# Two SwiGLU phases with five Strassen-Winograd pairs instead of four, the first pair's weight sums made earlier and kept in device memory

## The chip, the cores and the metric

One core of one Trainium2 chip. The metric is device time in microseconds (us) of one execution of the whole program. The engines named are those of the profile: PE (TensorE, matrix products), ACT (ScalarE), DVE (VectorE), POOL (GpSimd), and SP, which here only issues transfers.

## The reference

A decoder of two layers, 256 tokens of width 1024 in float32. Each layer is a half-step SwiGLU, an attention and another half-step SwiGLU: stick-breaking attention in the first layer, native sparse attention (NSA) in the second, whose keys and values are made between the layers. Cut to what the change touches:

```python
D_FF = -(-8 * D_MODEL // (3 * 256)) * 256      # 2816

def _swiglu(x, w_in, w_out):
    a, b = jnp.split(x @ w_in, 2, axis=-1)
    return (jax.nn.silu(a) * b) @ w_out

    for layer in range(DEPTH):
        h = h + 0.5 * _swiglu(_rmsnorm(h, ffn1_norm[layer]), ffn1_w_in[layer], ffn1_w_out[layer])
        hn = _rmsnorm(h, mix_norm[layer])
        ...
        h = h + 0.5 * _swiglu(_rmsnorm(h, ffn2_norm[layer]), ffn2_w_in[layer], ffn2_w_out[layer])
        if layer == N_A_LAYERS - 1:
            kvs = _nsa_shared_kv(h, kv_norm, nsa_w_kv, nsa_k_norm, ...)
    return h
```

## The kernel before

The program runs through phases in this order: f10 (first SwiGLU), stick (attention), f20 (second SwiGLU), kv (shared keys and values), f11 (third SwiGLU, with the compression of keys and values as side work), nsa (attention), f21 (fourth SwiGLU).

**Products.** A float32 product is made of three matmuls (`mm3`, L283 to L285): high part by high part, high by low, low by high. So each weight is split in two. A weight unit of 128x1024 (512 KB) is loaded by SP's queue into a ring of raw buffers (`ring`; five wraw, and three more in f10, f20 and f21), ScalarE copies its high part wh (L219), VectorE subtracts for the low part wl (L221), and the pair stands in a ring of six, two more in the phases named, until TensorE has read it. `pump` makes the next unit's split, `take` hands it out, `done` frees it, and `room` says how far ahead `pump` may go. The units are worked through in one list, `units`, written at build time in the order in which TensorE takes them.

**SwiGLU.** The 2816 columns are 11 blocks of 256, each with its gate columns beside it. A block made directly is 48 matmuls of 128x512 on 4 units. Its two gate products g (one per 128 tokens, L588 or L590) are then transposed (gTp, L598) and split into gTh and gTl (L604). The output product takes 22 chunks of 12 matmuls on one unit each, for which the transposed g must be there; its accumulators take four of the eight PSUM banks.

**Pairs.** Two blocks can be made as a pair, by the Strassen-Winograd scheme: seven products of 12 matmuls instead of eight, on sums of the inputs (`sums_of_h`, four subtractions hg at L646 to L649 and their splits, sums, at L644, once per phase) and on sums of weights. Of a pair's four weight tiles (two units each, b11, b12, b21, b22) products 1, 3 and 2 take b11, b22 and b21 as they are. Product 5 takes b11+b12, product 6 that plus b22, product 4 that plus b21, and product 7 b12+b22. VectorE makes the first three sums in tiles named keep (L229, six adds of 128x1024 per pair); the fourth comes from a plain load of b12 and an accumulating transfer of b22 on GpSimd's queue.

**Order.** Every engine's order is fixed at build time. `FAST` writes out a phase: a number is a direct block, a tuple is a pair with a pattern. In a pattern a digit is one of the seven products, c a chunk of the output product, m the transposes of one finished block, f and g the halves of a direct block inside a pair, s a step of side work, t and x the points where the transfers for product 7 of this pair and the next pair are issued. Blocks before the first tuple run first; chunks that no pattern holds run after the last pair. `chunk_order` gives the order in which blocks enter the output product.

## Time and profile before

| | us |
|---|---|
| median of 3 runs (lowest, highest) | 1001.96 (1001.72, 1002.34) |
| the profiled execution | 1002.48 |
| its span | 1000.7 |
| PE busy in it | 988.1 |
| DVE busy | 867.6 |
| ACT busy | 690.4 |
| POOL busy | 109.1 |

The TensorE clock granted was 1.0 throughout. A span is the time from the first to the last instruction of the profiled execution; what lies around it is 1.8 us. In the rows below, a row of a window gives its bounds and length, then the busy time and count of PE, PEld (weight loads), DVE, ACT and POOL, the granted clock, the share of the transfer engines and GB/s. A row of a timeline gives start and duration, engine, line, operation, output and inputs with their shapes, how many instructions in a row it holds, and in brackets the idle time before it with what ended it. A row of waits gives total, count and longest, in us. By TensorE's instructions f20 begins at 306.6, kv at about 483, f11 at 518, nsa at 714 and f21 at 822.

### The profile page before, as it was taken

The page shows a single profiled execution, that of the slowest core. Times are in us where ns is not written, and L with a number is a line of the kernel's source. Part 1 is how long each engine was busy: PE and PEld are TensorE (multiplying, and loading weights), DVE is VectorE, ACT ScalarE, POOL GpSimd, SP SyncE. Part 2 cuts the span into 40 slices and gives each one's busy share as a digit, 9 for nine tenths or more (in the row PEclk, how much of TensorE's full clock was granted, in tenths as well). Part 3 has the DMA queues.
Part 4 walks back from the last instruction along what each step waited for, and adds up shares of the span by engine and source line. Part 5 has one row for each costly group of instructions (what it writes and reads, how often), then busy time and mean ns, then how long its engine had stood idle before and what let it go on. Part 6 is the DMA issues. An engine that isn't in the chain of part 4 may idle for free.

```text
span 1000.7 us, 14046 instructions
## 1 busy us (share of the span) xinstructions
PE 988.1 (99%) x4985; PEld 822.2 (82%) x4985; DVE 867.6 (87%) x1157; ACT 690.4 (69%) x1083; POOL 109.1 (11%) x164
## 2 busy tenths in 40 slices
PE   9999999999999999999999999999999999999998
PEld 6787887899978888888887887888887888888887
DVE  7899999878869999997777788898799859999993
ACT  6676767577857677676565775666589857767771
POOL 0000000000000000000116400000046501000000
PEclk9999999999999999999999999999999999999999
DMA  9988774554336877665544584766350167687831
GB/s 333 346 245 254 227 219 136 178 171 131 125 124 231 265 238 231 234 190 175 198 156 154 196 301 148 227 211 211 119 187 23 43 224 213 204 248 229 244 110 43
DMA packets 55366, 193.67 MB, mean 194 GB/s; under 512 B 6272, under 2 KB 7296, under 8 KB 55296
## 3 DMA queue, kind: packets, MB, share of 16 engines
q1 hardware_dynamic: 51552, 180.03, 53.3%
q0 software_dynamic: 3456, 12.58, 7.3%
q8 instruction: 39, 0.64, 0.3%
q14 instruction: 31, 0.25, 0.1%
q10 hardware_dynamic: 288, 0.16, 0.1%
HBM read 191.70 MB, written 1.05 MB: 193 GB/s over the span
## 4 chain that ended last, share of the span: by engine, by line
PE 68%; issue 12%; DVE 7%; DMA 5%; ACT 4%; POOL 3%; SPq 0%; ACTq 0%; DVEq 0%; POOLq 0%
PE o L283 7%; PE o L285 6%; PE o L284 6%; PE c L283 5%; PE c L285 5%; PE c L284 5%; DVE wl L221 3%; DMA wraw<-in_f1i 2%; PE a L285 2%; PE a L283 2%; PE a L284 2%; PE cu L283 2%; PE cu L285 2%; PE cu L284 2%; DMA keep<-in_f1i 2%
## 5 line engine op out<-in xcount | busy, mean ns | idle before, releaser
L221 DVE TENSOR_TENSOR wl<-wraw,wh 128x1024 fp32r<-128x1024 f32 (+2 forms) x302 | 364.2, 1220 | 41.7 <-ACT wh L219 39.4
L219 ACT ACTIVATE wh<-wraw 128x1024 fp32r<-128x1024 f32 (+1 forms) x304 | 313.6, 1046 | 89.8 <-PE o L285 39.9
L219 ACT ACTIVATE wh<-keep 128x1024 fp32r<-128x1024 f32 x112 | 118.1, 1059 | 72.9 <-DVE keep L229 25.6
L221 DVE TENSOR_TENSOR wl<-keep,wh 128x1024 fp32r<-128x1024 f32 x112 | 133.9, 1220 | 11.1 <-ACT wh L219 10.4
L229 DVE TENSOR_TENSOR keep<-keep,wraw 128x1024 f32<-128x1024 f32 x80 | 97.5, 1219 | 2.5 <-DMA wraw<-in_f1i 1.9
L283 PE MATMUL o<-wh,gTh0f 128*128 128x512 f32 x192 | 76.4, 398 | 0.0
L284 PE MATMUL o<-wl,gTh0f 128*128 128x512 f32 x192 | 74.8, 390 | 0.0
L285 PE MATMUL o<-wh,gTl0f 128*128 128x512 f32 x192 | 74.7, 391 | 0.0
L283 PE MATMUL a<-wh,hT_f 128*128 128x512 f32 x176 | 69.9, 397 | 0.0
L285 PE MATMUL a<-wh,hT_f 128*128 128x512 f32 x176 | 68.9, 392 | 0.0
L284 PE MATMUL a<-wl,hT_f 128*128 128x512 f32 x176 | 68.6, 390 | 0.0
L283 PE MATMUL o<-wh,gTh1f 128*128 128x512 f32 (+1 forms) x160 | 63.7, 398 | 0.0
L284 PE MATMUL o<-wl,gTh1f 128*128 128x512 f32 (+1 forms) x160 | 62.0, 387 | 0.0
L285 PE MATMUL o<-wh,gTl1f 128*128 128x512 f32 (+1 forms) x160 | 61.3, 388 | 0.0
L441 POOL TENSOR_TENSOR rstd<-rss,mhalf 128x1 f32<-128x1 f32 x12 | 7.7, 642 | 376.2 <-DVE rss L439 376.2
L283 PE MATMUL c<-wh,hT_f 128*128 128x512 f32 x120 | 47.0, 391 | 0.0
L285 PE MATMUL c<-wh,hT_f 128*128 128x512 f32 x120 | 46.7, 389 | 0.0
L284 PE MATMUL c<-wl,hT_f 128*128 128x512 f32 x120 | 46.7, 389 | 0.0
L285 PEld LDWEIGHTS o<-wh,gTl0f 128*128 128x128 f32 x192 | 36.0, 188 | 8.0 <-DVE gTl0f L604 0.2
L283 PEld LDWEIGHTS o<-wh,gTh0f 128*128 128x128 f32 x192 | 36.1, 188 | 7.6 <-ACT vcBh L1233 0.3
L284 PEld LDWEIGHTS o<-wl,gTh0f 128*128 128x128 f32 x192 | 36.1, 188 | 7.1
L285 PEld LDWEIGHTS a<-wh,hT_f 128*128 128x128 f32 x176 | 33.0, 188 | 7.1
(352 smaller groups left out, 2439.3 us busy)
## 6 DMA issues: line engine op xcount, KB each, us to landing
wraw<-in_f1i SPq DMA_DIRECT2D x76, 512.0 KB, 4.5
wraw<-in_f2i SPq DMA_DIRECT2D x72, 512.0 KB, 4.5
wraw<-in_f1o SPq DMA_DIRECT2D x44, 512.0 KB, 4.6
wraw<-in_f2o SPq DMA_DIRECT2D x44, 512.0 KB, 4.8
wraw<-in_sbqk SPq DMA_DIRECT2D x16, 512.0 KB, 3.4
keep<-in_f2i SPq DMA_DIRECT2D x16, 512.0 KB, 4.2
keep<-in_f2i POOLq DMA_DIRECT2D x16, 512.0 KB, 5.5
keep<-in_f1i SPq DMA_DIRECT2D x12, 512.0 KB, 4.5
```

Source lines behind the costliest of these rows:

```text
L219: nc.scalar.activation(hi[:, 0:n], raw[:, 0:n], AF.Copy)
L221: e.tensor_tensor(lo[:, 0:n], raw[:, 0:n], hi[:, 0:n].bitcast(F32), op=OP.subtract)
L229: nc.vector.tensor_tensor(t, y, raw, op=OP.add)
L283: nc.tensor.matmul(o, xh, wh, start=start, stop=False, skip_group_check=True)
L284: nc.tensor.matmul(o, xh, wl, start=False, stop=False, skip_group_check=True)
L285: nc.tensor.matmul(o, xl, wh, start=False, stop=stop, skip_group_check=True)
L441: nc.gpsimd.tensor_tensor(r[:, 0:1], s, mhalf[:, 0:1], op=OP.pow)
```

## The change

f20 and f21 have made blocks 0, 1 and 4 directly (4 inside the first pair) and the pairs (2,3), (5,6), (7,8) and (9,10). They now make block 0 directly and the pairs (1,2), (3,4), (5,6), (7,8) and (9,10). f10 and f11 keep their patterns.

The first pair of f20 and of f21 reads all four weight sums (two units each, eight of 512 KB per phase) from tiles in device memory, as ordinary weight units. Its VectorE adds and its product 7's transfers go. The sums are made earlier:

- for f20 by transfers alone, during the attention (`early_sums`): 4 loads and 8 stores on SP's queue and 8 accumulating transfers on GpSimd's, through four tiles es, one step per `pump` from the twelfth unit of the attention on;
- for f21 by VectorE in kv and f11 (`Early` units, inserted in the unit list from the twelfth unit of kv on): 8 loads, 8 adds of 128x1024 (L191 after) and 8 stores.

Besides this, block 0 of f20 and f21 accumulates in the PSUM banks z, the keep tiles of f11 are opened before kv, and f21's raw ring starts at another place (`turn`). Over the whole program TensorE has 4954 matmuls instead of 4978, VectorE 414 splits instead of 402, 90 adds into keep instead of 84 and 6 into wraw instead of 4, and 32 adds x instead of 28, SP 398 transfers instead of 358 and GpSimd 32 instead of 24.

```diff
@@ -24,10 +24,10 @@
 LOW = 100
 
 
...
-        "f20": (0,1,(2, "1mft5tg36m7xx24", 4), (5,"mc1mccct5ct3cc67xx24"),(7,"mc1mct5ct3cc67xx24"),(9,"mc1mct5t3c6724")),
...
-        "f21": (0,1,(2, "1mft5tg36m7xx24", 4), (5,"mc1mccct5ct3cc67xx24"),(7,"mc1mct5ct3cc67xx24"),(9,"mc1mct5t3c6724"))}
...
+        "f20": (0,(1,"1m25c36m7xxc4"),(3,"m1cmct5t367xxcc24"),(5,"m1mct5t3c67xx24"),(7,"mc1cmt5cct3c67xx24"),(9,"m1mct5t3cc6724")),
...
+        "f21": (0,(1,"1m25c36m7xxc4"),(3,"m1mct5ct3c67xx24"),(5,"mc1mct5ct3c67xx24"),(7,"mc1mct5ct3c67xx24"),(9,"mc1mct5t3c6724"))}
 
 
 def chunk_order(l):
...
@@ -100,12 +107,15 @@
         self.raw, self.hi, self.lo = {}, {}, {}
         self.on_pool = ()
         self.keep, self.kept, self.missed, self.waiting, self.held = None, {}, 0, [], {}
-        self.limit = len(units)
+        self.limit, self.turn, self.owed = len(units), 0, 0
+        self.jobs, self.jobs_from = [], 0
         self.spans, self.extra = [], None
         self.nr = self.nl = self.ns = self.nt = self.nd = 0
 
     def ring(self, u):
-        more = self.extra is not None and self.wide(u) and self.nr % 8 in (1, 4, 7)
+        if self.spans and u == self.spans[-1][0]:
+            self.turn = 6 - self.nr
+        more = self.extra is not None and self.wide(u) and (self.nr + self.turn) % 8 in (1, 4, 7)
         pool, b = (self.extra, 3) if more else (self.pool, self.raws)
         self.nr += 1
         return pool.tile([P, 1024], F32, tag="xraw" if more else "wraw", bufs=b, name=f"wraw{u}")
@@ -127,7 +137,7 @@
         if self.nl >= len(self.units):
             return
         x = self.units[self.nl]
-        if not isinstance(x, Sum):
+        if not isinstance(x, (Sum, Early)):
             self.load_part(0, 1)
             return
         if self.keep is None:
@@ -173,11 +183,35 @@
     def apart(self, u):
         return any(i + 6 <= u < j and (u - i) % 4 == 3 for i, j in self.spans)
 
+    def skip(self, u):
+        return u < len(self.units) and isinstance(self.units[u], Early)
+
+    def early(self, x, u):
+
+        add = lambda t, y: self.nc.vector.tensor_tensor(t, t, y, op=OP.add)
+        k, keep = self.kept[x.key], None
+        y = self.raw.pop(u, None)
+        if x.step == 1:
+            keep, self.held[x.key] = self.held[x.key], y
+            add(keep, y)
+        elif x.step == 2:
+            add(k, self.held.pop(x.key))
+        else:
+            add(k, y)
+            if x.step == 0:
+                self.held[x.key] = y
+            else:
+                del self.kept[x.key]
+        self.nc.sync.dma_start(x.store, k if keep is None else keep)
+
     def room(self, u, slack):
-        if u >= self.nd + self.bufs + 2 * self.wide(u) - slack:
+        if self.skip(u):
+            return True
+        early = sum(self.skip(v) for v in range(self.nd, u))
+        if u >= self.nd + self.bufs + 2 * self.wide(u) - slack + early:
             return False
         n = sum(self.apart(v) for v in range(self.nd, u))
-        return n < 2 if self.apart(u) else u - self.nd - n < self.bufs
+        return n < 2 if self.apart(u) else u - self.nd - n - early < self.bufs
 
     def pair_of(self, u):
         if self.apart(u):
@@ -206,6 +240,18 @@
         while self.nl <= u:
             self.load()
         nc = self.nc
+        if self.skip(u):
+            prio = self.tc.cur_priority
+            self.tc.cur_priority = prio + low
+            self.early(x, u)
+            self.tc.cur_priority = prio
+            self.ns += 1
+            self.owed += 1
+            if x.step > 1:
+                while self.owed:
+                    self.load()
+                    self.owed -= 1
+            return True
         n = x.shape[-1] if isinstance(x, bass.AP) else 1024
         hi, lo = self.hi[u], self.lo[u] = self.pair_of(u)
         if not isinstance(x, Sum):
@@ -235,13 +281,20 @@
         self.tc.cur_priority = prio
         self.ns += 1
         self.load()
+        if self.jobs and u >= self.jobs_from:
+            self.jobs.pop(0)()
         return True
 
     def done(self, n=1):
 
-        self.nd += n
+        for _ in range(n):
+            while self.skip(self.nd):
+                self.nd += 1
+            self.nd += 1
 
     def take(self):
+        while self.skip(self.nt):
+            self.nt += 1
         u = self.nt
         while self.ns < u + 1:
             assert self.pump(0)
@@ -286,6 +339,49 @@
 
 
     units = []
+    dr = ctx.enter_context(tc.tile_pool(name="dr", bufs=1, space=bass.MemoryType.DRAM))
+    stored = {}
+
+    def store(l, n):
+
+        j = [e[0] for e in FAST[l] if isinstance(e, tuple)][n]
+        stored[l, j] = [[dr.tile([P, 1024], F32, name=f"s{l}{j}{y}{i}") for i in range(2)] for y in range(4)]
+
+    def early_units(l):
+
+        j = next(j for x, j in stored if x == l)
+        at = stored[l, j]
+        v = []
+        for i in range(2):
+            b = lambda y, k: a[l[:2] + "i" + l[2]][4 * (j + y) + 2 * k + i]
+            key = ("p", "t", i)
+            v += [Early(key, 0, at[0][i], b(0, 0), b(1, 0)), Early(key, 1, at[1][i], None, b(1, 1)),
+                  Early(key, 2, at[2][i]), Early(key, 3, at[3][i], None, b(0, 1))]
+        return v
+
+    def early_sums(pool, l, j):
+
+        at = stored[l, j]
+        b11, b12, b21, b22 = [[a[l[:2] + "i" + l[2]][4 * (j + y) + 2 * k + i] for i in range(2)]
+                              for k in range(2) for y in range(2)]
+        x, y = [[pool.tile([P, 1024], F32, tag=f"es{z}{i}", bufs=1, name="es") for i in range(2)] for z in range(2)]
+
+        def move(*pairs):
+            for t, src in pairs:
+                for i in range(2):
+                    tc.keep_in_program_order(nc.sync.dma_start(t[i], src[i]))
+
+        def plus(*pairs):
+            for t, src in pairs:
+                for i in range(2):
+                    nc.gpsimd.dma_start(t[i], src[i], accum_op=OP.add)
+
+        jobs = []
+        for gap, f, *y_ in zip((1, 1, 1, 2, 2, 2, 1, 3, 1, 4), (move, move, plus, plus, move, plus, move, move, plus, move),
+                             (((x, b11),), ((y, b12),), ((x, b12),), ((y, b22),), ((at[0], x),), ((x, b22),), ((at[1], y),),
+                              ((at[2], x),), ((x, b21),), ((at[3], x),))):
+            jobs += [lambda: None] * (gap - 1) + [lambda f=f, z=y_[0]: f(*z)]
+        return jobs
 
     def fast(l):
 
@@ -307,18 +403,22 @@
             z = pairs.index(j)
             b11, b21, b12, b22 = b(j, 0), b(j, 1), b(j + 1, 0), b(j + 1, 1)
             key = [(j, "t", i) for i in r]
+            at = stored.get((l, j))
             third = lambda z, i: (pairs[z], 2, i)
             kept = lambda last=False: [Sum(key[i], last=last) for i in r]
-            plus = [(third(z, i), b22[i], True) for i in r]
+            plus = [(third(z, i), b22[i], True) for i in r] if at is None else []
             own = l != "f11"
             ahead = []
-            if own and z == 0:
+            if own and z == 0 and at is None:
                 for i in r:
                     also(i - 2, (third(0, i), b12[i], False))
-            if own and z + 1 < len(pairs):
+            if own and z + 1 < len(pairs) and (l, pairs[z + 1]) not in stored:
                 ahead = [(third(z + 1, i), b(pairs[z + 1] + 1, 0)[i], False) for i in r]
             for ch in pat:
-                if ch == "1":
+                if at is not None and ch in "1536724":
+                    x = {"1": b11, "3": b22, "2": b21, "5": at[0], "7": at[1], "6": at[2], "4": at[3]}[ch]
+                    v += [Unit(x[i]) for i in r]
+                elif ch == "1":
                     v += [Unit(b11[i], key=key[i], of=third(z, i)) if own else Sum(key[i], load=b11[i], join=b12[i])
                           for i in r]
                 elif ch in "56":
@@ -356,13 +456,18 @@
         fast(l)
         spans.append((n, len(units)))
 
+    store("f20", 0)
+    store("f21", 0)
+
     wide("f10")
 
     units[0:8] = [units[4 * (i % 2) + i // 2] for i in range(8)]
+    st0 = len(units)
     for i in range(2):
         units.extend(a["sbv"][j] for j in range(4 * i, 4 * i + 4))
         units.extend(a["sbqk"][j] for j in range(8 * i, 8 * i + 8))
     add("sbo"), wide("f20")
+    kv0 = len(units)
     add("kv")
     f1i1 = fast("f11")
     units.extend(f1i1[:4 * CMP_J])
@@ -372,6 +477,11 @@
         units.extend(f1i1[4 * CMP_J + 2 * i:4 * CMP_J + 2 * i + 2])
     units.extend(f1i1[4 * CMP_J + 8:])
     add("nsi0"), add("nsi1")
+    k = kv0 + 12
+    for i, x in enumerate(early_units("f21")):
+        k += (0, 2, 2, 2)[i % 4]
+        units.insert(k, x)
+        k, cw = k + 1, cw + 1
     nso = len(units)
     add("nso"), wide("f21")
     W = Weights(tc, wp, units, raws=5, bufs=6)
@@ -778,7 +888,7 @@
                 twin()
             else:
                 for j in range(j0):
-                    o = accs("a")
+                    o = accs("a") if j or l == "f11" else [zbank("a") for _ in range(2)]
                     for i, f in enumerate(proj_block(512, hT, j == 0, post, o)):
                         f()
                         if j and i == 1:
@@ -852,6 +962,8 @@
             vp = [sp.tile([P, 2, 8, P], R, name=f"vp{i}") for i in range(2)]
             rB = sp.tile([P, 512], F32, name="rBqk")
             qkT, z, spx, wx = {}, {}, {}, {}
+            W.jobs = [f for l, j in stored if l == "f20" for f in early_sums(sp, l, j)]
+            W.jobs_from = st0 + 12
 
             def v_evac(i, o):
                 for t in range(2):
@@ -1575,6 +1687,7 @@
         fp1 = st["fp"] = fes.enter_context(ffn_pool("f11"))
         qg = st["qg"] = kp.tile([P, DH], F32, name="qg")
         nc.vector.tensor_scalar(qg, vec[:, V_QN:V_QN + DH], 0.125, None, op0=OP.mult)
+        W.open(fp1)
         side = kv_phase(n3, rs, post, st)
         n5 = HT("m1")
         rs, post = ffn("f11", n4, rs, post, [(5, n5)], side, fp1,
```

VectorE at the start of f20's first pair, before. hg and sums are the sums of inputs, wl a unit's low part, keep a weight sum, gTl0f the low part of transposed gates, g a gate product:

```order
L649 SCALAR_TENSOR_TENSOR hg<-hg 128x512
L644 TENSOR_TENSOR sums<-hg,sums 128x512 x3
L221 TENSOR_TENSOR wl_3374<-wraw_3327,wh_3373 128x1024
L221 TENSOR_TENSOR wl_3388<-wraw_3347,wh_3387 128x1024
L229 TENSOR_TENSOR keep<-keep,wraw_3327 128x1024
L604 TENSOR_TENSOR gTl0f_3446<-gTp,gTh0f_3445 128x512
L229 TENSOR_TENSOR keep<-keep,wraw_3347 128x1024
L221 TENSOR_TENSOR wl_3406<-wraw_3361,wh_3405 128x1024
L590 TENSOR_TENSOR g<-a_3397,sil 128x256
L221 TENSOR_TENSOR wl_3422<-wraw_3379,wh_3421 128x1024
L221 TENSOR_TENSOR wl_3435<-keep,wh_3434 128x1024
```

The same place after:

```order
L759 SCALAR_TENSOR_TENSOR hg<-hg 128x512
L754 TENSOR_TENSOR sums<-hg,sums 128x512 x3
L267 TENSOR_TENSOR wl_3412<-wraw_3369,wh_3411 128x1024
L714 TENSOR_TENSOR gTl0f_3483<-gTp,gTh0f_3482 128x512
L267 TENSOR_TENSOR wl_3424<-wraw_3387,wh_3423 128x1024
L267 TENSOR_TENSOR wl_3459<-wraw_3399,wh_3458 128x1024
L700 TENSOR_TENSOR g<-c_3450,sil 128x256
L267 TENSOR_TENSOR wl_3471<-wraw_3415,wh_3470 128x1024
L267 TENSOR_TENSOR wl_3493<-wraw_3427,wh_3492 128x1024
L267 TENSOR_TENSOR wl_3505<-wraw_3462,wh_3504 128x1024
L267 TENSOR_TENSOR wl_3522<-wraw_3474,wh_3521 128x1024
```

The keep adds are gone, and splits stand in their place.

VectorE in kv, around the statistics kss of the keys (kvb is the keys' work tile, Vl a small low part of the values):

```order
L457 TENSOR_TENSOR hT_f_5008<-hg,hT_f_5008 128x4x128
L1071 SCALAR_TENSOR_TENSOR Vl<-kv_5082,rstd,Vh 128x2x64
L646 TENSOR_TENSOR hg<-hg 128x512
L221 TENSOR_TENSOR wl_5179<-wraw_5125,wh_5178 128x1024
L1071 SCALAR_TENSOR_TENSOR Vl<-kv_5083,rstd,Vh 128x2x64
L1092 TENSOR_REDUCE kss<-kvb 128x16
L1071 SCALAR_TENSOR_TENSOR Vl<-kv_5083,rstd,Vh 128x2x64
L1093 TENSOR_SCALAR kss<-kss 128x16
L221 TENSOR_TENSOR wl_5205<-wraw_5137,wh_5204 128x1024
```

After:

```order
L1183 SCALAR_TENSOR_TENSOR Vl<-kv_5156,rstd,Vh 128x2x64
L191 TENSOR_TENSOR keep<-keep,wraw_5280 128x1024
L1183 SCALAR_TENSOR_TENSOR Vl<-kv_5157,rstd,Vh 128x2x64
L267 TENSOR_TENSOR wl_5275<-wraw_5260,wh_5274 128x1024
L1183 SCALAR_TENSOR_TENSOR Vl<-kv_5157,rstd,Vh 128x2x64
L1204 TENSOR_REDUCE kss<-kvb 128x16
L267 TENSOR_TENSOR wl_5295<-wraw_5262,wh_5294 128x1024
L1205 TENSOR_SCALAR kss<-kss 128x16
L191 TENSOR_TENSOR keep<-keep,wraw_5264 128x1024
```

Between the two kss instructions a wl stands now instead of a Vl, and early adds (L191) before and after.

VectorE further on, around hT_xb, which GpSimd's work on kvb and ScalarE release:

```order
L221 TENSOR_TENSOR wl_5321<-wraw_5220,wh_5320 128x1024
L1154 TENSOR_TENSOR hT_xb<-kvb,hT_xb 128x16x64
L221 TENSOR_TENSOR wl_5333<-wraw_5267,wh_5332 128x1024
L221 TENSOR_TENSOR wl_5382<-wraw_5279,wh_5381 128x1024
L604 TENSOR_TENSOR gTl0f_5344<-gTp,gTh0f_5343 128x512
L590 TENSOR_TENSOR g<-a_5300,sil 128x256
L221 TENSOR_TENSOR wl_5394<-wraw_5324,wh_5393 128x1024
L590 TENSOR_TENSOR g<-a_5301,sil 128x256
```

After:

```order
L267 TENSOR_TENSOR wl_5419<-wraw_5404,wh_5418 128x1024
L756 TENSOR_TENSOR hg<-hg 128x512
L757 TENSOR_TENSOR hg<-hg 128x512
L1266 TENSOR_TENSOR hT_xb<-kvb,hT_xb 128x16x64
L758 SCALAR_TENSOR_TENSOR hg<-hg 128x512
L267 TENSOR_TENSOR wl_5464<-wraw_5430,wh_5463 128x1024
L267 TENSOR_TENSOR wl_5486<-wraw_5432,wh_5485 128x1024
L714 TENSOR_TENSOR gTl0f_5442<-gTp,gTh0f_5441 128x512
L759 SCALAR_TENSOR_TENSOR hg<-hg 128x512
L700 TENSOR_TENSOR g<-a_5392,sil 128x256
L267 TENSOR_TENSOR wl_5528<-wraw_5467,wh_5527 128x1024
L700 TENSOR_TENSOR g<-a_5393,sil 128x256
```

Two hg now stand ahead of hT_xb that stood earlier, and two behind it, ahead of the first g.

More of the change, by code (lines that the diff above doesn't have):

```diff
@@ L24 @@
 LOW = 100
-FAST = {"f10": (0, 1, 2, (3, "cccm1ctc5ct367xx24"), (5,"mc1mct5ct3c67xx24"),(7,"mc1mct5ct3c67xx24"),(9,"mc1mct5t36724")),
[3 rows of a table removed]
+FAST = {"f10": (0,1,2,(3,"cccm1ctc5ct367xx24"),(5,"mc1mct5ct3c67xx24"),(7,"mc1mct5ct3c67xx24"),(9,"mc1mct5t36724")),
[3 rows of a table added]
 def chunk_order(l):
@@ L91, in __init__ @@
         self.more = ()
+class Early:
+    def __init__(self, key, step, store, load=None, join=None):
+        self.key, self.step, self.store, self.load, self.join = key, step, store, load, join
 class Weights:
```

2 rows, old and new, of the table FAST are left out of this document.

## The prediction

> **What bounds the kernel now.** First the engines' busy shares, then the chain that ended last, then TensorE's list of waits.
>
> ```profile
> PE 988.1 (99%) x4985; PEld 822.2 (82%) x4985; DVE 867.6 (87%) x1157; ACT 690.4 (69%) x1083; POOL 109.1 (11%) x164
> PE 68%; issue 12%; DVE 7%; DMA 5%; ACT 4%; POOL 3%; SPq 0%; ACTq 0%; DVEq 0%; POOLq 0%
> PE gTp L598 <- DVE g L590: 1.0, 1, 1.0
> PE n L284 <- DVE wl L221: 0.9, 1, 0.9
> PE c L283 <- ACT cp L686: 0.4, 1, 0.4
> ```
>
> TensorE is busy in 988.1 of the span's 1000.7 us, and its waits are single ones of a microsecond or less. It bounds the kernel, so matmuls that go are time that goes, as long as VectorE, second at 87%, keeps the weights split ahead of it. By stretches (columns: length, then busy time of PE, PEld, DVE, ACT and POOL, clock, DMA share, GB/s) the cover is thinner than 87% suggests:
>
> ```profile
> 306.60:466.80 160.20, 160.19 (x728) 131.90 (x727) 156.17 (x171) 116.39 (x145) 7.91 (x9) 1.00 0.75 233
> 822.05:980.50 158.45, 158.44 (x720) 130.49 (x719) 152.79 (x167) 113.74 (x141) 7.99 (x9) 1.00 0.68 203
> 94.18:174.09 79.91, 79.53 (x357) 64.19 (x357) 77.81 (x88) 58.33 (x74) 3.52 (x4) 1.00 0.68 199
> 391.48:425.18 33.70, 33.70 (x154) 27.74 (x153) 32.67 (x34) 24.28 (x29) 1.72 (x2) 1.00 0.77 234
> 383.32:388.76 5.44, 5.44 (x26) 4.50 (x25) 3.93 (x5) 2.13 (x2) 0.00 (x0) 1.00 0.79 270
> ```
>
> The first two are the changed phases f20 and f21: VectorE is busy for 156.17 of 160.20 and 152.79 of 158.45 us, and TensorE still never waits. The third is three pairs of the unchanged f10, the fourth one pair of f20, the fifth two products of it.
>
> **Matmuls.** The last window holds 24 starts of 128x512 matmuls (two more only touch its edges), so 5.44/24 = 0.2267 us each. Two blocks alone are 2 x 48 of them; as a pair they are 7 x 12 = 84. Each phase turns blocks 1 and one other from direct into a pair, so each saves 12 x 0.2267 = 2.72 us: 5.44 us in both. The transposes stay, four per pair. This is all that the change can give.
>
> **VectorE's queue against TensorE's.** The cost is in what VectorE must do per microsecond of TensorE.
>
> ```profile
> 571.24 5.75 DVE L221 TENSOR_TENSOR wl<-wraw,wh 128x1024 fp32r<-128x1024 f32 x5
> 320.70 1.89 DVE L644 TENSOR_TENSOR sums<-hg,sums 128x512 fp32r<-128x512 f32 x3
> 548.19 0.42 DVE L590 TENSOR_TENSOR g<-a,sil 128x256 f32<-128x256 f32 x1
> 322.50 2.35 DVE L221 TENSOR_TENSOR wl<-wraw,wh 128x1024 fp32r<-128x1024 f32 x2
> 329.69 0.39 PE L284 MATMUL c<-wl,hT_f 128*128 128x512 f32 x1
> ```
>
> Five splits end to end take 5.75 and one alone 1.22 (2.35 for two), so one costs (5.75 - 1.22)/4 = 1.135 in a full queue; a 128x512 add (1.89 for three) 0.60; a g of 0.42 alone about 0.335 in the same way. A steady pair then costs VectorE 14 splits and 6 weight sums (22.7), two transfers x, four g and two gTl (3.74), and one split per chunk c of the output product: 26.4 + 1.135c. TensorE takes 7 x 2.72 + 0.72 for transposes + 2.72c = 19.8 + 2.72c. They are even at about 4.2 chunks. A phase has 22 chunks: before, four pairs shared them; now five do, so the pairs hold fewer each. In f20 they hold 2, 4, 2, 5 and 3, in f21 2, 3, 4, 4 and 3. The first pair makes no sums (its stored ones are loaded like weights), so it is VectorE's easiest: 21.9 us against 25.2.
>
> I laid VectorE's instructions in the order's sequence end to end at these costs beside TensorE's, and took the lead: when TensorE first reads a unit, less when its split ends. On the kernel before this gives 6.18 us where the last two rows give 329.69 - (322.50 + 1.22) = 5.97. After the change a direct block less stands ahead of f20's first pair (48 x 0.2267 = 10.9 us of TensorE, 4 x 1.135 + 2 x 0.335 + 0.60 = 5.8 of VectorE), and the same lead comes to 0.74 us. The easy first pair then raises it. In f20 the stretches of the four later pairs take VectorE 31.9, 28.4, 32.1 and 30.5 us, TensorE 30.65, 25.2, 33.4 and 28.25. The leads at their starts are 4.99, 3.71, 0.54 and 1.78, and at the tail -0.49, with -0.76 the lowest. In f21 the stretches are 29.5, 29.85, 32.7 and 30.8 against 27.9, 30.6, 30.6 and 27.6, the leads 7.54, 5.95, 6.74 and 4.67, 1.45 at the tail, 0.05 once.
>
> How far VectorE falls behind such a sum f10 shows: laid end to end its stretch is 77.6 us of VectorE and took 79.91, so 2.3 us slip away in waits for ScalarE's wh. TensorE ran there with leads of 0.7 to 3 us and lost 79.91 - 79.53 = 0.4. In f20 the last 62 us run at low lead: 62/79.9 x 2.3 = 1.8 slip, and 0.49 is missing already, so **+2.3** (0 if it goes as in f10; 5 if the slip runs from the phase's start, 160/79.9 x 2.3 = 4.6 upon -0.49). In f21 1.45 of lead absorbs most of it: f10's own loss, **+0.4** (0 to 3).
>
> **f21's early sums: eight adds in kv and f11.** VectorE has room there by share, but kv holds a serial chain over GpSimd:
>
> ```profile
> 483.00:547.30 64.30, 64.30 (x303) 53.11 (x302) 47.20 (x66) 36.67 (x54) 23.41 (x29) 1.00 0.54 177
> 518.96 2.51 POOL L1090 TENSOR_TENSOR kvb<-kva 128x1024 f32<-128x1024 f32 x1 [30.78 <-ACT kva L1065]
> 521.49 1.22 DVE L1092 TENSOR_REDUCE kss<-kvb 128x16 f32<-128x1024 f32 x1 [1.52 <-POOL kvb L1090]
> 522.89 0.87 DVE L1093 TENSOR_SCALAR kss<-kss 128x16 f32<-128x16 f32 x1
> 523.84 3.28 POOL L1095 TENSOR_TENSOR ksr<-kss,mhalf 128x16 f32<-128x16 f32 x1
> 528.13 2.39 DVE L649 SCALAR_TENSOR_TENSOR hg<-hg 128x512 f32<-128x512 f32 x1
> 538.27 3.31 POOL L1149 TENSOR_TENSOR kvb<-kvb,vec 128x120 f32<-128x120 f32 x8
> 542.71 1.23 DVE L1154 TENSOR_TENSOR hT_xb<-kvb,hT_xb 128x1024 fp32r<-128x1024 f32 x1 [7.33 <-ACT hT_xb L1153]
> 543.85 2.35 DVE L221 TENSOR_TENSOR wl<-wraw,wh 128x1024 fp32r<-128x1024 f32 x2
> 548.66 0.55 PE L598 MATMUL gTp<-cst,g 128*128 128x128 f32 x3 [1.04 <-DVE g L590]
> ```
>
> VectorE idles 7.33 us ahead of hT_xb, then TensorE waits 1.04 for the g behind it: the chain into hT_xb has no slack, and whatever stands between hT_xb and that g is paid. By the order two hg (L758, L759) now stand there, at some 0.6 each in a full queue: +1.2. Between the two kss instructions stood a small Vl of some 0.26, now a split of 1.135: +0.9, on the chain. Sum **+2.1**. The lower end is 1.2, if the kss step finds another cover; the upper 5.5, if the three adds put between 518 and 541 (3 x 1.135) also delay it.
>
> That GpSimd can be slowed by VectorE a row bears on: its L1149 adds took 3.31 us here while VectorE idled, and 6.62 in the next group, while VectorE ran splits:
>
> ```profile
> 548.96 6.62 POOL L1149 TENSOR_TENSOR kvb<-kvb,vec 128x120 f32<-128x120 f32 x8 [7.38 <-ACT kvb L1138]
> ```
>
> [...]
>
> **f20's early sums: transfers alone, beside the attention.**
>
> ```profile
> 200.00:302.00 102.00, 100.69 (x735) 91.50 (x734) 79.92 (x133) 75.22 (x142) 0.00 (x0) 1.00 0.42 136
> 15.00:25.00 10.00, 10.00 (x44) 7.77 (x43) 10.00 (x16) 8.09 (x15) 0.00 (x0) 1.00 1.04 402
> keep<-in_f2i POOLq DMA_DIRECT2D x16, 512.0 KB, 5.5
> keep<-in_f1i POOLq DMA_DIRECT2D x8, 512.0 KB, 9.0
> wraw<-in_f2i SPq DMA_DIRECT2D x72, 512.0 KB, 4.5
> SPq L122 <- DVE wl L221: 484.5, 196, 25.0
> ```
>
> 4 loads, 8 accumulating transfers and 8 stores of 0.524 MB go through a stage whose transfer engines are 42% busy. At the page's shares per byte (53.3% for 180.03 MB, 7.3% for 12.58) they add some 43 us of 102, to about 84%. SP issues the stores in the queue of the weight loads, each behind an accumulation of 5.5 to 9.0 us; SP waits for VectorE's splits 196 times anyway, because the loads run a ring of five ahead. Six split pairs and five raw buffers at 102/32 = 3 us per unit cover 9 us. GpSimd computes nothing in that window. I take **0** (0 to 1). The eight accumulations add no VectorE work. Block 0's sums in other PSUM banks, the pool opened before kv and the ring's changed turn cost nothing that a row shows: in all three the loads are early.
>
> **Sum.** -5.44 + 2.3 + 0.4 + 2.1 + 0 = -0.64 us on the profiled execution of 1002.48 (span 1000.7 and 1.8 around it): 1001.84. The median of the runs shown, 1001.96, lies 0.5 lower, so I forecast **1001.3**. The runs go from 1001.72 to 1002.34; under 0.2%, 2.0 us, no change can be told.
>
> **Rivals.**
> A, faster: VectorE keeps up as it does in f10, where leads of 0.7 to 3 us cost 0.4. Then both phases lose 0.5 together: -5.44 + 2.1 + 0.5 = -2.8, 999.1. If kv also costs only its 1.2, 998.2. For it: TensorE does not wait anywhere in f20 with VectorE 97% busy. Against it: leads below zero cannot be made up.
> B, slower: GpSimd's chain from 519 to 541 is lengthened by the three early adds in its way, 3 x 1.22 less one hg of 0.69, so 3.0 more: kv 5.1, the sum +2.4, 1004.3. It decides once kv costs over some 4.7 us.
> C, slower: raw weights come late in f20's first pair. It loads 16 units in its 25 us, the stored sums among them: 16 x 0.524/24.5 = 342 GB/s against 402, the most that a row shows; accumulations for the next pair land there too. Where these take 9.0 instead of 4.5, +4.5: 1005.2. Against it: loads run ahead across block 0.
>
> **Chances.** The forecast (within 0.2% of before) 0.43, A 0.34, B 0.15, C 0.08. So faster 0.34, same 0.43, slower 0.23. The range goes from A with the cheap kv, 998.2, to B with a little of C, 1004.8. The forecast's own is 1000.0 to 1003.5.
>
> **What the next profile would show.** TensorE's matmuls fewer by 24; VectorE above 98% busy in f20's pairs with splits as TensorE's last wait, near the last two pairs; in f21 hardly any. In kv the wait of gTp for g grown from 1.0 to about 3, with the two hg ahead of that g. In the attention no wait of TensorE for transfers. A gTp wait still near 1.0 and no split waits would mean A; one above 5 with longer GpSimd steps B; waits for wraw right after block 0 of f20 C. The forecast is also wrong if VectorE's slip in f20 grows with its load rather than with time.

## The result

The changed kernel takes 1009.8 us (median of 6 runs, 1008.15 to 1012.51) against 1001.9 for the kernel before (6 runs, 1000.94 to 1002.34): a ratio of 1.0084 with a 95% interval of 1.0074 to 1.0094. It is 0.8% slower, clear of the spread of the runs. The forecast was 1001.3 with a range from 998.2 to 1004.8. Its profiled execution took 1008.6 with a span of 1006.8, so 1.2 us of the median stand in no profile; the runs also spread over 4.4 us, those of before over 1.4.

First the busy shares and TensorE's waits over the whole kernel, after:

```profile
PE 987.0 (98%) x4961; PEld 820.2 (81%) x4961; DVE 891.9 (89%) x1181; ACT 701.4 (70%) x1103; POOL 116.6 (12%) x172
PE gTp L708 <- DVE g L700: 5.5, 2, 4.5
PE c L336 <- ACT cu L789: 1.4, 2, 0.8
PE xtp L1246 <- ACT kvb L1250: 0.9, 1, 0.9
PE kTp L1229 <- DVE hid L1290: 0.7, 1, 0.7
PE o L337 <- DVE wl L267: 0.3, 1, 0.3
PE c L336 <- ACT cp L796: 0.2, 1, 0.2
```

The wait for g that was 1.0 is 5.5 in two pieces. Splits that TensorE waits for in the pairs come to 0.3. Where the time went is read from the first matmul of each phase in the two timelines (us from the span's start; the last column is what the stretch up to the next phase gained or lost):

| stretch | begins before | begins after | change in it |
|---|---|---|---|
| f10 | 0 | 0 | -0.94 |
| attention | 185.50 | 184.56 | -0.03 |
| f20 | 306.60 | 305.63 | -0.18 |
| kv and f11 | 483.02 | 481.87 | +8.22 |
| nsa | 714.35 | 721.42 | +0.71 |
| f21 | 822.05 | 829.83 | -1.64 |
| end of span | 1000.7 | 1006.8 | |

f10 is the same program before and after; among the runs below its length differs from that of before by -0.94 to +1.31, so its 0.94 is no effect of the change. The phases that were changed behave about as forecast: f20 even (forecast -0.4), f21 a little faster (forecast -2.3). kv and f11 lose 8.2 us, the whole loss and more. nsa's 0.71 comes and goes with TensorE's clock (experiment 4).

GpSimd's chain in kv, after:

```profile
517.80 2.81 POOL L1202 TENSOR_TENSOR kvb<-kva 128x1024 f32<-128x1024 f32 x1 [30.48 <-ACT kva L1177]
524.38 3.82 POOL L1207 TENSOR_TENSOR ksr<-kss,mhalf 128x16 f32<-128x16 f32 x1 [0.28 <-DVE kss L1205]
531.11 4.75 POOL L1217 TENSOR_TENSOR kva<-kva,vec 128x256 f32<-128x256 f32 x4
540.73 3.30 POOL L1261 TENSOR_TENSOR kvb<-kvb,vec 128x120 f32<-128x120 f32 x8
```

The row of its kva before:

```profile
530.05 4.25 POOL L1105 TENSOR_TENSOR kva<-kva,vec 128x256 f32<-128x256 f32 x4
```

From the start of kvb to that of the eight L1261 adds it took 538.27 - 518.96 = 19.31 us before and takes 540.73 - 517.80 = 22.93: 3.62 more. VectorE's and TensorE's ends of the chain, after:

```profile
517.64 1.23 DVE L191 TENSOR_TENSOR keep<-keep,wraw 128x1024 f32<-128x1024 f32 x1 [0.80 <-DMA wraw<-in_f2i]
519.04 2.65 DVE L267 TENSOR_TENSOR wl<-wraw,wh 128x1024 fp32r<-128x1024 f32 x1
521.88 1.21 DVE L1204 TENSOR_REDUCE kss<-kvb 128x16 f32<-128x1024 f32 x1
523.01 1.21 DVE L267 TENSOR_TENSOR wl<-wraw,wh 128x1024 fp32r<-128x1024 f32 x1
529.52 2.59 DVE L191 TENSOR_TENSOR keep<-keep,wraw 128x1024 f32<-128x1024 f32 x1
545.15 1.23 DVE L1266 TENSOR_TENSOR hT_xb<-kvb,hT_xb 128x1024 fp32r<-128x1024 f32 x1 [6.65 <-ACT hT_xb L1265]
546.29 0.68 DVE L758 SCALAR_TENSOR_TENSOR hg<-hg 128x512 f32<-128x512 f32 x1
549.77 0.68 DVE L759 SCALAR_TENSOR_TENSOR hg<-hg 128x512 f32<-128x512 f32 x1
550.84 0.48 PE L708 MATMUL gTp<-cst,g 128*128 128x128 f32 x1 [4.50 <-DVE g L700]
```

A split of 2.65 and an add of 2.59, each alone, took twice their 1.22, and GpSimd's kvb, ksr and kva beside them got longer too (2.51 to 2.81, 3.28 to 3.82, 4.25 to 4.75). The long split also stands ahead of kss, which begins 1.27 us after kvb has ended (520.61 to 521.88); before, it began at once (521.47 to 521.49). Then the two hg stand in the way as forecast. Behind the wait something new, in windows of 3.41 us (the clock is the third number from the right):

```profile
547.29:550.70 3.41, 0.00 (x0) 0.00 (x0) 3.41 (x5) 2.02 (x4) 0.00 (x0) 1.00 0.44 165
550.71:554.12 3.41, 1.38 (x4) 0.68 (x4) 3.02 (x6) 2.13 (x3) 0.00 (x0) 0.50 0.72 193
554.12:557.53 3.41, 3.38 (x10) 2.90 (x11) 0.15 (x1) 2.19 (x3) 1.67 (x4) 0.50 1.00 401
557.54:560.95 3.41, 3.41 (x16) 2.77 (x15) 3.34 (x3) 1.58 (x3) 1.66 (x2) 1.00 0.74 264
762.33:765.74 3.41, 1.94 (x14) 1.56 (x13) 3.40 (x9) 3.41 (x15) 3.08 (x7) 1.00 0.00 0
765.75:769.16 3.41, 3.41 (x13) 2.40 (x12) 3.41 (x8) 3.26 (x14) 2.38 (x6) 0.50 0.00 0
```

TensorE idled 4.5 us, and its granted clock was a half from 550.71 to 557.53; the 128x512 matmuls there start 0.43 us apart (555.49, 555.91, 556.34) instead of 0.23 (558.06, 558.29, 558.52). It was a half once more in nsa, from 765.75 to 769.16, where no wait was longer than 1.3 us. The clock over the whole run is 0.995, before 1.0.

### The profile page after: what moved, and what is told of

It reads as the page before. It is cut to its first block, busy times and chain, and to the rows that moved or that the text cites. A ratio compares the mean times of both kernels' runs of the same rounds, so it can differ in the third digit from the quotient of the medians.

```text
span 1006.8 us, 14115 instructions
## 1 busy us (share of the span) xinstructions
PE 987.0 (98%) x4961; PEld 820.2 (81%) x4961; DVE 891.9 (89%) x1181; ACT 701.4 (70%) x1103; POOL 116.6 (12%) x172
## 3 DMA queue, kind: packets, MB, share of 16 engines
HBM read 208.48 MB, written 9.44 MB: 216 GB/s over the span
## 4 chain that ended last, share of the span: by engine, by line
PE 63%; issue 14%; DVE 8%; ACT 6%; DMA 5%; POOL 3%; SPq 0%; ACTq 0%; POOLq 0%; DVEq 0%
PE o L337 6%; PE o L336 6%; PE o L338 6%; PE c L336 5%; PE c L338 5%; PE c L337 5%; DVE wl L267 3%; ACT wh L265 2%; PE cu L336 2%; PE cu L338 2%; PE cu L337 2%; PE qk L990 2%; DMA wraw<-in_f2i 1%; PE qk L991 1%; PE qk L992 1%
## 5 line engine op out<-in xcount | busy, mean ns | idle before, releaser
L267 DVE TENSOR_TENSOR wl<-wraw,wh 128x1024 fp32r<-128x1024 f32 (+2 forms) x314 | 380.4, 1229 | 34.9 <-ACT wh L265 33.4
L265 ACT ACTIVATE wh<-wraw 128x1024 fp32r<-128x1024 f32 (+2 forms) x316 | 323.3, 1044 | 82.0 <-PE o L338 30.3
L336 PE MATMUL c<-wh,hT_f 128*128 128x512 f32 x144 | 56.9, 395 | 1.4 <-ACT cu L789 1.4
L336 PE MATMUL a<-wh,hT_f 128*128 128x512 f32 x144 | 57.8, 401 | 0.0
L338 PE MATMUL a<-wh,hT_f 128*128 128x512 f32 x144 | 56.9, 395 | 0.0
L337 PE MATMUL a<-wl,hT_f 128*128 128x512 f32 x144 | 56.7, 394 | 0.0
L337 PE MATMUL c<-wl,hT_f 128*128 128x512 f32 x144 | 56.4, 392 | 0.0
L338 PE MATMUL c<-wh,hT_f 128*128 128x512 f32 x144 | 56.2, 390 | 0.0
L336 PE MATMUL cu<-wh,sums 128*128 128x512 f32 x112 | 44.6, 399 | 0.0
L336 PE MATMUL c<-wh,sums 128*128 128x512 f32 x112 | 44.2, 395 | 0.3 <-ACT cp L796 0.2
L338 PE MATMUL cu<-wh,sums 128*128 128x512 f32 x112 | 43.8, 391 | 0.0
L337 PE MATMUL cu<-wl,sums 128*128 128x512 f32 x112 | 43.7, 390 | 0.0
L338 PE MATMUL c<-wh,sums 128*128 128x512 f32 x112 | 43.7, 390 | 0.0
```

The costliest lines, as they stand in the source:

```text
L265: nc.scalar.activation(hi[:, 0:n], raw[:, 0:n], AF.Copy)
L267: e.tensor_tensor(lo[:, 0:n], raw[:, 0:n], hi[:, 0:n].bitcast(F32), op=OP.subtract)
L336: nc.tensor.matmul(o, xh, wh, start=start, stop=False, skip_group_check=True)
L337: nc.tensor.matmul(o, xh, wl, start=False, stop=False, skip_group_check=True)
L338: nc.tensor.matmul(o, xl, wh, start=False, stop=stop, skip_group_check=True)
```

## The experiments

Every kernel below is compared with the kernel before, run on the same chip at the same time (1002.2 to 1002.6). "Lost in f11" means kv and f11 together, by first matmuls as in the table, against the one profile of before.

**1. Which part.** Only f20, and only f21 (with its early adds):

```diff
-        "f21": (0,(1,"1m25c36m7xxc4"), ...     # f20 alone: f21's line as before, no Early units
-        "f20": (0,(1,"1m25c36m7xxc4"), ...     # f21 alone: f20's line as before, no early transfers
```

> Only f20 has five pairs, with its sums by transfers during the attention; f21 is as before, without early adds. K: f20 gives back all but 0.2 to 0.5 us, and kv is as before: 1001 to 1002. L: the same. V: f20 alone costs, 1003 to 1005.

Measured: 1002.63, ratio 1.0008 (0.9998 to 1.0017), no difference; f20 -0.52 us, attention -0.03. The transfers beside the attention cost nothing, and f20 gives back most of its 2.72. V's 1003 to 1005 did not come; the time lies just above K's.

> Only f21 has five pairs, with the early adds in kv; f20 is as before. K: kv and f11 +7 to +9, f21 -1.7, so 1007 to 1010. L: the same. V: half of the loss, 1004 to 1006.

Measured: 1011.69, ratio 1.0095 (1.0080 to 1.0110); +9.53 lost in f11, f21 -1.26. The loss belongs to f21's half of the change (the time lies above K's 1007 to 1010).

**2. Adds or transfers.** The loads and stores stay, the adds go:

```diff
-        add = lambda t, y: self.nc.vector.tensor_tensor(t, t, y, op=OP.add)
+        add = lambda t, y: None
```

> The eight early adds are left out, their loads and stores stay (f21's first pair then works on unsummed weights). K: the loss in kv is gone, 999 to 1001.5. L: the transfers cost as before, 1006 to 1009. V: no change, 1008 to 1012.

Measured: 1002.17, ratio 0.9993 (0.9984 to 1.0003), f11 -0.28, the clock at 1.0. So the 8 us in kv come with the adds, with which VectorE's order is gone too: without them all four hg stand ahead of hT_xb again. Rival L, that the transfers by themselves make the weights late, falls at this place. But the kernel is not faster than before, where K had 999 to 1001.5: f20 is +0.50 here and f21 -0.15.

**3. Why the adds slow GpSimd.** A reduction of the same length that reads one tile, at the same place in VectorE's order:

```diff
-        add = lambda t, y: self.nc.vector.tensor_tensor(t, t, y, op=OP.add)
+        add = lambda t, y: self.nc.vector.tensor_reduce(t[:, 0:16], y.rearrange("p (n d) -> p n d", d=64), ...)
```

> Each of the eight early adds is replaced by a VectorE reduction of the loaded tile, which reads one tile instead of two and takes about as long; its place in VectorE's order, the loads and the stores stay (the stored sums are then not the sums). Theory H (a two-input VectorE instruction and a GpSimd instruction hold each other up): GpSimd's steps from kvb to the eight L1261 adds take 1 to 2 us less than in the changed kernel, TensorE's wait for g falls from 4.5 to 2 to 3.5 us, the time to 1003 to 1006. Theory O (only the order on VectorE counts): the wait stays at 4 to 5 us, 1008 to 1011.

Measured: 1007.49, ratio 1.0050 (1.0035 to 1.0066). GpSimd's chain in this kernel:

```profile
518.08 1.90 POOL L1203 TENSOR_TENSOR kvb<-kva 128x1024 f32<-128x1024 f32 x1 [30.47 <-ACT kva L1178]
523.74 2.91 POOL L1208 TENSOR_TENSOR ksr<-kss,mhalf 128x16 f32<-128x16 f32 x1 [0.28 <-DVE kss L1206]
529.44 3.86 POOL L1218 TENSOR_TENSOR kva<-kva,vec 128x256 f32<-128x256 f32 x4
538.11 3.30 POOL L1262 TENSOR_TENSOR kvb<-kvb,vec 128x120 f32<-128x120 f32 x8
```

538.11 - 518.08 = 20.03 us against 22.93: of the 3.62 us that the chain grew, 2.9 go when the adds become reductions, 0.7 stay with the order. TensorE's first wait there is 1.6 us instead of 4.5, the same 2.9. So O falls: the adds themselves lengthen the chain, as H has it. That their second input does it is not shown: the reduction also writes 16 columns instead of 1024, and no run parts the two. Nor is one input always harmless: VectorE's pair of copies kva, one input each, takes 1.24 us beside GpSimd's kva (L1218 here, L1105 before) and 0.48 to 0.49 elsewhere, in this kernel and before.

The time still misses H's 1003 to 1006, since f11 loses 7.26: waits of 1.6, 1.1 and 1.3 follow within 5 us with four transposes between, and the clock halves all the same, for 3.41 us (0.998 over the run). The third of them points at a second cost of the eight instructions. These are ScalarE's waits for f11's weights from 483 to 600, before, after, without the adds and with the reductions:

```profile
ACT wh L219 <- DMA wraw<-in_f1i: 2.1, 3, 1.7
ACT wh L265 <- DMA wraw<-in_f1i: 13.1, 9, 2.6
ACT wh L265 <- DMA wraw<-in_f1i: 0.8, 3, 0.4
ACT wh L266 <- DMA wraw<-in_f1i: 12.9, 9, 2.7
```

The loads and stores alone make no weight late (0.8), loads and stores with eight instructions on VectorE do, one input or two. In the changed kernel one such wait of 2.65 us stands ahead of the copy kvb for which TensorE waits at xtp. By which path, the stores that wait for an add in SP's queue or the raw buffers that an add holds, these two runs do not show.

**4. The clock.** Two, four and nine reductions of a PSUM tile put ahead of that g in the kernel before:

```diff
                         if i == 2:
+                            if l == "f11" and j == 1:
+                                for _ in range(4):
+                                    nc.vector.tensor_reduce(lag, o[0].rearrange("p (n d) -> p n d", d=32), ...)
                             gate(j, 0, o)
```

> The kernel before, with two reductions of a PSUM tile ahead of the g in kv. With four the first wait was 4.1 us and the clock fell. Theory C: with two it is 2.4 to 3.2 us, the clock stays at 1.0, and the span grows by the wait alone, 2.5 to 3.5 us, to 1004.5 to 1006. If any wait costs the clock, some 2 us more.

> The kernel before, with four reductions of a PSUM tile (some 0.65 us each) put on VectorE ahead of the g in kv for which TensorE waits. Theory C: the wait grows by 2 to 3 us to under 3.4, the clock stays at 1.0, the span grows by just that, 1003.5 to 1005.5. Were the clock to drop for any wait, 2 us more.

> The same with nine reductions. Theory C: the wait grows to 5 to 8 us, the clock falls to a half after it, and the span grows by 1.5 to 3.5 us more than the wait does: 1008 to 1013. Without C it grows by the wait alone, 1006 to 1009.

Measured, with two, four and nine: 1004.73 (ratio 1.0033, 1.0018 to 1.0048), 1009.74 (1.0073, 1.0053 to 1.0093) and 1008.33 (1.0059, 1.0039 to 1.0079). TensorE's waits in kv and f11, in that order of kernels:

```profile
PE gTp L598 <- DVE g L590: 2.2, 1, 2.2
PE xtp L1138 <- ACT kvb L1142: 0.6, 1, 0.6
...
PE gTp L598 <- DVE g L590: 5.5, 2, 3.9
...
PE xtp L1138 <- DVE kva L1135: 5.3, 1, 5.3
```

With two, the waits grew from 1.3 (gTp 1.0, kTp 0.3) to 2.8, f11 lost 1.69, and the clock stayed at 1.0 there. With four they are 5.5, 4.2 more, and f11 lost 6.86; with nine 5.3, 4.0 more, and f11 lost 6.22 (TensorE then takes the transposes xtp first and waits for a copy kva behind the reductions). In both the clock stood at 0.5 for 6.83 us; with four:

```profile
554.00:556.00 2.00, 2.00 (x9) 1.90 (x10) 2.00 (x2) 1.14 (x3) 2.00 (x2) 0.50 0.73 201
558.00:560.00 2.00, 2.00 (x7) 1.53 (x6) 0.02 (x1) 1.06 (x1) 0.85 (x3) 0.61 0.88 346
```

So in kv a wait of 2.2 us cost its length, one of 3.9 or 5.3 some 2.2 to 2.7 us more. (With four the first wait was longer than I expected, since a split was ordered behind the reductions.) By the same reckoning the changed kernel lost 8.22 with waits of 7.1 instead of 1.3: 5.8 are waits, 2.4 are left for the clock.

The length of a wait does not decide alone. In the kernel with two reductions the clock fell in nsa, for 3.41 us (0.998 over the run, 1.00 in every window from 540 to 570), and nsa lost 0.82. Four of these profiles have such a fall there, and nsa loses 0.71 to 0.84 in them; in the others that leave nsa alone it is -0.18 to +0.25, with the same waits of 1.3 us at most. Nor does TensorE's busy share ahead of a fall decide: in nsa of the changed kernel it was busy for 1.94 of the 3.41 us ahead (the row 762.33:765.74 above), and in nsa of the kernel before for 1.95 of the 3.41 us from 754.95 to 758.36, and there the clock stayed at 1.0. The wait of 2.2 us, from 547.2 to 549.4, left it at 1.0 too. No run shows what decides, nor the limits of length in these expectations, 3.4 us with four reductions and some 3 us in the second filler below: behind 2.2 us there was no fall, behind 3.8 us (the first filler) and more there was one, and so there was behind three waits of 1.6 us at most.

Filling the changed kernel's wait with matmuls was to take that part away:

```diff
+                if l == "f11" and j == 1:
+                    for _ in range(14):
+                        nc.tensor.matmul(p, hT[0][:, 0, 0:P], hT[0][:, 0:2, :], start=True, stop=True, ...)
```

> The changed kernel with 14 more matmuls of 128x512 (3.2 us) issued by TensorE just ahead of the transposes that wait for g; their output is overwritten. Theory C (a TensorE idle for 4.5 us runs at half clock afterwards, and this costs 2 to 3 us): the granted clock stays at 1.0 there, the wait falls to some 1.3 us, the time by 2 to 3 us to 1006.5 to 1008. Without C the time stays the same, 1009 to 1011, since the matmuls only fill the wait.

> As the kernel with 14 more matmuls of 128x512 ahead of the transposes that wait for g, but their output goes to a PSUM bank that nobody else uses at that time, so that they do run in the wait. Theory C (TensorE idle for longer than some 3 us costs it half its clock for several us): the granted clock stays at 1.0 from 540 to 570, TensorE's wait falls from 4.7 to some 1.5 us, and the time falls by 1.5 to 2.5 us to 1007 to 1008.5. Without C: 1009 to 1011.

Measured: 1011.03 (1.0087, 1.0072 to 1.0102) and 1011.49 (1.0094, 1.0080 to 1.0108). Both missed. The first wrote into gTp's own bank, which VectorE frees by a gTl0f that stands behind hT_xb, so the matmuls waited 3.8 us themselves, and the clock stood at a half behind that for 3.41 us. In the second they ran, but TensorE then waited 1.6, 1.1 and 1.3 us from 552 to 557 with only transposes between, and the clock halved at 557.2, for 3.41 us. f11 lost 8.24 and 9.44. What the clock costs in the changed kernel is thus inferred from the reductions, not removed.

**5. Another place for f21's sums.** Behind both hT_xb, in f11; spread out there; and with the stores on GpSimd's queue:

```diff
-    k = kv0 + 12
+    k = kv0 + 32
-        k += (0, 2, 2, 2)[i % 4]
+        k += (0, 1, 1, 1)[i % 4]          # the two later kernels: (0, 2, 2, 2)
...
-        self.nc.sync.dma_start(x.store, ...)
+        self.nc.gpsimd.dma_start(x.store, ...)    # the third alone
```

> The early adds of f21 are moved behind both hT_xb of the key chain (20 units later, one unit apart); all else is as changed. Theory K (the adds in kv lengthen the serial chain over GpSimd, TensorE waits 4.5 us and then runs at half clock): kv and f11 fall from +8.2 us to +0.5 to +1.5, the time to 999 to 1001. Rival L (the 16 added transfers on SP's queue make f11's weights late): they are all still there, 1005 to 1009. Rival V (VectorE in the five pairs): nothing changes, 1008 to 1012.

> The early adds behind both hT_xb as in the kernel that lost 14 us in f11, but two units apart instead of one. If the loss there came from transfers too dense for SP's queue and the raw ring (theory D): f11 loses 3 to 8 us less, 1008 to 1012. If from the place (the raw buffers that an add holds, next to the compression's units): still 14, 1015 to 1017.

> The same, with the eight stores issued on GpSimd's queue instead of SP's, so that no weight load stands behind a store that waits for an add. Theory S (the stores block SP's queue): f11 loses 0 to 3 us, 1000 to 1004. Without S as the kernel with the stores on SP's queue.

Measured: 1016.36 (1.0138, 1.0116 to 1.0160), 1019.78 (1.0177, 1.0160 to 1.0195) and 1013.27 (1.0108, 1.0090 to 1.0126); f11 lost 13.98, 18.75 and 13.16. kv's order was that of before in all three and its wait for g 1.0 to 1.2, but now TensorE waits for splits. In the first:

```profile
PE a L336 <- ACT wh L265: 7.1, 3, 3.9
...
ACT wh L265 <- DMA wraw<-in_f1i: 10.4, 6, 5.5
```

So K's forecast for the first failed, and its loss went beyond L's too: the place in kv is bad, but this one is worse. Spreading made it worse, and moving the stores took back 5.6 of 18.75, where S had all but 0 to 3: D falls, S holds for less than a third. What is left I would put down to the raw buffers: an early load takes one of the five, and the first two of each half's three are held until the next add has read them. That was not tried by itself.

Transfers alone inside device memory during nsa, the second kernel with product 5 ahead of product 2 in the first pairs:

```diff
+        def plus(t, src):                       # t a tile sf: no VectorE, no SBUF
+            for i in range(2):
+                nc.gpsimd.dma_start(t[i], src[i], accum_op=OP.add, max_dma_last_dim=2048)
-(1,"1m25c36m7xxc4")
+(1,"15m2c36m7xxc4")                             # the second kernel
```

> Both phases with five pairs, but f21's sums are made by transfers alone inside device memory during the projections of nsa (8 copies on SP's queue, 8 accumulations on GpSimd's); no early add on VectorE, kv as in the kernel before. Theory K: kv and f11 cost nothing more, f20 gives 0 to -0.5, f21 -1 to -1.7, nsa 0 to +1: 999.5 to 1002. Rival L: the transfers cost in nsa what they cost in kv, 1004 or more.

> The same, with the first pair's products in the order 1, 5, 2 instead of 1, 2, 5 in f20 and f21, so that ScalarE's copy cu of product 1 (for which TensorE waited 0.9 and 1.1 us ahead of product 2) has a product's time. If that wait is ScalarE's full queue at the first pair: 1 to 2 us less than the kernel without it, 998 to 1000.5. If VectorE's splits bound there: no difference.

Measured: 1030.72 (1.0296, 1.0269 to 1.0322) and 1033.57 (1.0299, 1.0283 to 1.0316). nsa lost 28.7 and 32.8, so K missed, and the loss went far beyond L's 1004. The accumulations into device memory go one at a time: each is issued some 0.3 us after the one ahead of it has landed (716.26, 724.20 and 730.06 in the first kernel), though it goes into another tile and the copies into all four had landed by 712.74. GpSimd's rstd stands behind them:

```profile
724.54 0.90 POOL L398 DMA_DIRECT2D sf<-in_f2i  x1 [6.99 <-issue]
730.39 0.90 POOL L398 DMA_DIRECT2D sf<-in_f2i  x1 [4.95 <-issue]
731.97 0.56 POOL L564 TENSOR_TENSOR rstd<-rss,mhalf 128x1 f32<-128x1 f32 x1
...
DVE rstd L565 <- POOL rstd L564: 15.3, 1, 15.3
```

Later in nsa TensorE waited 10.4 us for a P of GpSimd's that stands behind two more of them. Whether the chip or the program's own semaphores make the accumulations go singly, no run shows.

The new order did remove the wait for cu (its two waits, 1.4 in all, are not in the second kernel's list), but f21 was then +0.18 instead of -0.72, with a wait of 1.8 for a copy cp late in the phase. In this one pair of profiles it shifted the wait, and gained nothing.

At last all sums during the attention, f20's as in the change and f21's inside device memory:

> Both phases with five pairs, and all early sums by transfers during the attention, beside which f20's sums cost nothing: f21's by 8 copies and 8 accumulations inside device memory, mixed with f20's. No early add on VectorE, no early transfer in kv, f11 or nsa. If only the place counted: attention 0 to +0.5, f20 0 to -0.5, kv and f11 0, f21 -0.5 to -1.6, so 1000 to 1002 against some 1002.3 before. If SP's or GpSimd's queue fills there (20 MB more in 120 us): attention or f20 +2 to +10, 1003 to 1011.

Measured: 1011.2 (1.0090, 1.0075 to 1.0104). The attention lost 9.15 with the transfer engines 97% busy (76% in the changed kernel), one wait of TensorE of 5.9 us and the clock at a half for 10.2; f20 gave -1.03, f11 -0.26, f21 -1.29. That is the second half of the expectation. No place for f21's sums made the kernel faster than before.

**6. Who gives the saved products back.** On top of the kernel without early adds, the weight-sum adds of f20's and f21's later pairs cut to 64 columns:

```diff
-            nc.vector.tensor_tensor(t, y, raw, op=OP.add)
+            nc.vector.tensor_tensor(t[:, 0:m], y[:, 0:m], raw[:, 0:m], op=OP.add)    # m = 64 in f20 and f21
```

> On top of the kernel without the early adds: in f20's and f21's later pairs the weight-sum adds on VectorE work on 64 of 1024 columns (a GpSimd memset fills the tile), so that VectorE has some 20 us less to do in each phase; the sums are not the sums. If VectorE's full queue is what gives the saved products back (theory V2), f20 and f21 give most of 5.4 us: -2 to -2.7 each, 996.5 to 999. If it is the turn from TensorE to ScalarE and back, which every pair has (theory T), they stay near 0 and the time at 1001 to 1003.

Measured: 1000.29, ratio 0.9978 (0.9970 to 0.9987). f20 -0.37, f21 -1.62, where the kernel without early adds has +0.50 and -0.15. By the medians, 1.9 us apart, VectorE's load takes back some 2 of the 5.4 us, between the two theories; by these two profiles it is 2.3. Where it takes them back they do not show: in the ten other kernels with five pairs in both phases and the same order of products, f20 and f21 together came to anything from -2.32 to +0.35, and the changed kernel, with its full adds, has -0.18 and -1.64, about as much as the light one. What stays in every one of them, light or not, is this place, here in f20 of the changed kernel:

```profile
319.61 1.14 ACT L753 ACTIVATE sums<-hg 128x512 fp32r<-128x512 f32 x2
320.64 0.59 ACT L789 ACTIVATE cu<-c 128x512 f32<-128x512 f32 x1
```

TensorE's last matmul of product 1 runs from 319.61 to 320.0. ScalarE, with the input sums and splits of a phase that reaches its pairs a block sooner, copies cu only from 320.64 to 321.23, and a matmul of product 2 starts 0.9 us late in f20 and 1.1 in f21 (by the starts of matmuls; the list, which counts idle time alone, has 1.4 for both). In the light kernel it is 0.8 and 1.1. The kernel before made a half of the direct block 4 right behind product 1 (the f of its pattern), which gave that copy its time. VectorE's part shows under ScalarE's name too; in the kernel without early adds, in f21:

```profile
959.85 2.01 ACT L265 ACTIVATE wh<-keep 128x1024 fp32r<-128x1024 f32 x2 [1.89 <-DVE keep L275]
963.57 1.06 ACT L265 ACTIVATE wh<-keep 128x1024 fp32r<-128x1024 f32 x1 [1.71 <-DMA keep<-in_f2i]
964.53 0.58 ACT L796 ACTIVATE cp<-c 128x512 f32<-128x512 f32 x1
```

wh waits for a sum on VectorE, then for the accumulating transfer of product 7, and cp, for which TensorE waits 1.1 us, stands behind both. In the changed kernel's f21 this wait is not there.

## Why the prediction was wrong

- **Matmuls, -5.44.** Right: 24 fewer, and each phase's gain has to be read against 2.72.
- **f20, +2.3.** Right in size: f20 gained 0.18, so 2.54 were given back (1.7 to 3.6 in the other kernels with the same order of products). The cause was only half right. TensorE's rows name ScalarE's copies, of which the one wait for cu is 0.9, and how much of it is VectorE's queue the run with light pairs does not settle (some 2 us over both phases, by the medians). The lead that I laid end to end left ScalarE's queue out. Two small figures in it were off as well: the split is 1.13 by its rows, not 1.135, and the first lead 1.1 by the terms beside it (6.18 - 10.9 + 5.8), not 0.74.
- **f21, +0.4.** Too small: 2.72 - 1.64 = 1.08, nearly all of it the one wait for cu (1.09 by the starts of matmuls), for which the sum had no term. The size is this profile's; in the other kernels f21 ran from -1.44 to -0.11.
- **Early transfers in the attention, 0.** Right (-0.03).
- **kv, +2.1.** This step failed: 8.22. The two hg cost their 1.2 (first g minus hT_xb is 5.22 us as against 4.01 before, by starts). The split between the two kss cost 0.15 instead of 0.9 (kss to ksr 2.50 as against 2.35); the long split ahead of kss cost 1.25, which no term had. But above all the sum let the early adds fall into VectorE's idle 7.33 us at no cost, where they lengthen GpSimd's chain; that was rival B, which I priced at 5.1 in all and gave 0.15. The chain grew by 3.6 where B had 3.0 on top of 0.9. That each add holds the chain for the whole of its 1.22 us, which is B's 3.0, no run shows; what the runs show is that 2.9 of the 3.62 us go with reductions of the same length in the adds' place. Then no case held what follows a long wait, the halved clock (2.4 us by the reckoning above), nor the later waits of xtp and kTp (0.9, and 0.7 instead of 0.3), the first behind a late weight. The upper bound of 5.5 added up VectorE's work and left these out.
- **Rival A** was refuted: with kv undisturbed the kernel is even with before (0.9993), not 2.8 us faster. **Rival C** did not come: TensorE has no wait for wraw in f20's first pair (ScalarE waited 2.0 us for the stored sums there). Its time was added up wrongly besides: 4.5 on 1001.3 is 1005.8, not 1005.2.
- The range to 1004.8 ended at B. What stood in the rows and was not drawn on is the clock: the kernel before has no wait of over 1.3 us after its start, so its clock of 1.0 said nothing of longer ones. Why it stayed at 1.0 in nsa too, with TensorE busy there for 1.95 of 3.41 us where the changed kernel had 1.94 ahead of its fall, no run shows.

## What to carry to other kernels

Before work is put into an engine's idle time, look for whom that engine's neighbour works then: here VectorE's adds beside a GpSimd chain left it 3.62 us longer, reductions of the same length in their place 0.7, and one of the adds took 2.59 us instead of 1.22; with the loads and stores around them ScalarE waited 13.1 us for f11's weights instead of 2.1. Price a TensorE wait by its length, and look at the granted clock behind it: here a wait of 2.2 us cost its length, waits of 3.9 and 5.3 us cost 2.2 to 2.7 us more at half the clock, and a fall in nsa, where no wait is over 1.3 us, some 0.8. And a saving on the bounding engine is worth only as much as the second and third queue can follow: 24 matmuls were saved, 5.4 us, of which f20 and f21 gave back 3.6 in the changed kernel and all in the one without early adds.
